# TensorE fed from the start, attention's two ends and the last row rearranged, in a hybrid decoder block

## The chip, the cores and the metric

The kernel runs on one core of one Trainium2 chip. The metric is the device time of one execution in microseconds; of several runs the median counts. The core has a matrix engine (TensorE, "PE" in the profile, with "PEld" for its loading of weights), three engines for element-wise work (VectorE "DVE", ScalarE "ACT", GpSimd "POOL") and a queue engine (SyncE "SP") that issues most of the transfers (DMA). Each engine works through its own list of instructions in order.

## The reference

One decoder block on x of 1024 positions by 1024 channels, all in float32. A conditioning vector c gives six modulation vectors (shift, scale and gate, twice). A normalised and modulated x is projected to an S5 input u, to q, k, v and to two gates; an S5 state-space branch and an attention branch run side by side, are merged by the gates, and a SwiGLU feed-forward part follows.

```
mod = silu(c) @ w_ada + b_ada                  -> sh1, sc1, g1, sh2, sc2, g2
h = rmsnorm(x, norm1_g) * (1 + sc1) + sh1
u, q, k, v, gate_a, gate_b = split(h @ w_in)
y_a = s5_branch(u) @ w_a                       # scan over 1024 steps, then a GLU
y_b = stick_breaking_attention(q, k, v) @ w_b
x = x + g1 * ((sigmoid(gate_a) * y_a + sigmoid(gate_b) * y_b) @ w_o)
h = rmsnorm(x, norm2_g) * (1 + sc2) + sh2
x = x + g2 * ((silu(h @ w_ffn_gate) * (h @ w_ffn_up)) @ w_ffn_down)
out = rmsnorm(x, norm_f_g)

# attention, 8 heads of 64; strictly causal
z = q @ k.T / 8 ;  mask = key < query
log_not = where(mask, log_sigmoid(-z), 0)
suffix  = sum of log_not over the later keys
weights = where(mask, exp(log_sigmoid(z) + suffix), 0)
out     = weights @ v
```

## The kernel before, in words

Most matrix products are done as three products of split operands: each float32 operand is cut into a high and a low part (the high part by a copy on ScalarE or GpSimd, the low part by a subtraction on VectorE or GpSimd), and TensorE adds high x high, high x low and low x high. Weights come in through `weight` (L442): a load, the two splits, and a ring of buffers (`wring`) whose next use has to wait for the products of the one before.

The work is written as a sequence of stages. A scheduler sets the order of the instructions on each engine by a simulated timeline; in the stage `start` the order is the written one, and in attention all matrix products are pinned to the written order (`pinned`, L832).

1. `start` (L563): SyncE loads x, the columns of w_in for u, and the first third of w_ada, in the order in which they are used. The row norms are worked out (`square`, `rstd`, `scale`); `turn` (L640) transposes x on TensorE against the identity; `small` transposes the small parameters; `ada_products` (L609) and `ada_sums` (L617) make the first modulation vectors, in four groups g of 256 columns: 32 products, a copy on ScalarE, and four products with one column. `modulate` turns the transposed x into h, and `product` forms u. The steps of the S5 parameters go on VectorE beside it.
2. The S5 branch, with the projection to v and gate_a on TensorE beside it, and the rest of w_ada multiplied by c on VectorE (`ada_rest`, L991), whose partial sums are stored to memory as `aD`.
3. The GLU of the S5 branch, the projections to q and k of the first pair of heads, and `branch_a` (L1070): product with w_a, times the sigmoid of gate_a (`gt`), result `na` stored as `nD`; the last of `ada_rest` runs beside it.
4. `attention` (L942). 40 units: four pairs of heads, two halves of the queries, and blocks of 128 keys from late to early. A unit has three steps: `scores` (L875: z = q k on TensorE, a mask addition on the diagonal ones on VectorE, a softplus on ScalarE and VectorE, split into `wh` and `wl`), `sums` (L906: suffix sums by products with a triangle and with ones, the running row kept in `row0` and `row1`; then an exponential), and `values` (L932). `scores` of a unit is written three units ahead (LOOK). Between the steps go single products of `fillers` (L836): the jobs in JOBS are the projections to q and k of the later pairs of heads and to gate_b, 48 products each, handed out 8 after the sums, 8 after the scores, and 12 after each of the first three scores (FILL). What is left over runs behind the last unit. A job's weights are loaded two jobs ahead (AHEAD). `triangles` (L818) builds the triangle and the mask on GpSimd just before attention.
5. `branch_b` (L1090): product with w_b, merge with gate_b and `nD`. Its accumulators go round eight PSUM banks (`banks`). `ada_row` spreads g1; `ada_cols` (L1022) makes the second shift and scale, 16 products with one column from `aD`.
6. `attend_out` (w_o, residual, second norm, transposes), and the feed-forward part `ffn` with `gate_up` and `down`, whose products are arranged as in Strassen's method.
7. The last rows (L1448 on): for each of eight blocks of 128 rows the last products, the residual, the sum of squares, and `close` (L1436), which takes the root (`rstd_p`, `rstd_s`) and scales the row. The last block is done in two halves: after the first half, two GpSimd steps (L1467) prepare the root and a third (L1468) multiplies the left half of the row by the norm's weights.

SBUF buffers come from pools that are laid out from the left and from the right. A new pool lies where closed ones lay, and its first writes wait for their last users. Before attention, the pools `tri` and `work` are opened after the stage `branch_a` has closed its pool `ar2`, which holds `gt`, `na` and the partial sums of `ada_rest`.

Of the kernel before, what the change touches and what calls it, by code (L numbers as in the profile page):

```python
# [365 lines left out]
KT = 8  # L366
# [12 lines left out]
FILL = (8, 8, 12)  # L379
JOBS = (("q", 1), ("k", 1), ("g", 0), ("g", 1), ("q", 2), ("k", 2), ("g", 2), ("q", 3), ("k", 3), ("g", 3), ("g", 4), ("g", 5), ("g", 6), ("g", 7))  # L380
# [49 lines left out]
class Block:  # L430
# [132 lines left out]
    def start(self, const, up, s5p):  # L563
# [8 lines left out]
        with self.pool("s0", 1, side="right") as sp, self.pool("s0a", 1, side="right") as ap, self.pool("s5t", 1, side="right") as st, \  # L572
# [66 lines left out]

            def turn(h, k):  # L640
                q = turned[h, k] = tp.tile([P, 512], F32, name="tp")
                for t in range(4):
                    nc.tensor.transpose(q[:, P * t:P * t + P], x[4 * h + t][:, P * k:P * k + P], self.ident)
# [192 lines left out]
    def fillers(self, qk, qp, kp, gp):  # L836

        nc = self.nc
# [4 lines left out]
        def load(j):  # L843
            n, i = jobs[j]
            c0 = {"q": 512, "k": 1024, "g": 3072}[n] + P * i
            loaded.append(self.w3(self.weight(self.in_cols(c0), lo_eng=nc.gpsimd, hi_eng=nc.gpsimd if n == "g" else None, ring=rings[j % 3])))
# [3 lines left out]
        for j, (n, i) in enumerate(jobs):  # L850
            if j + AHEAD < len(jobs):
                load(j + AHEAD)
            if n != "g":
                t = (qp if n == "q" else kp).tile([P, 1024], F32, name=n)
                qk[i][n == "k"] = t
# [19 lines left out]
    def scores(self, u, qk, work):  # L875
# [18 lines left out]
        if diag:  # L894
            m = P * (2 - len(u.kbs))
            nc.vector.tensor_tensor(a, z, self.mask[:, m:m + f].unsqueeze(1).broadcast_to([P, 2, f]), ALU.add)  # L896
        else:
            nc.scalar.copy(a, z)
# [43 lines left out]
    def attention(self, qk, qp, kp, vp, op, gp, work):  # L942
# [5 lines left out]
        for n in range(RWB):  # L948
            t = work.tile([P, 2, 512], F32R, name=f"row{n}")
            nc.vector.tensor_scalar(t.rearrange("p a (b c) -> p (a b) c", c=P), self.ident.unsqueeze(1).broadcast_to([P, 8, P]), 0.0, None, ALU.mult)  # L950
            carries.append(t)
# [6 lines left out]
        fill = self.fillers(qk, qp, kp, gp)  # L958
# [6 lines left out]
        for i in range(-LOOK, len(units) + 1):  # L965
# [56 lines left out]
    def ada_cols(self, const, tp, pp):  # L1022

        nc = self.nc
        ps = pp.tile([P, 512], F32, name="pa")
        for a in range(2):
            t = tp.tile([P, 1024], F32, name="ac")
            nc.sync.dma_start(out=t.rearrange("p (a b) -> p a b", a=2), in_=self.aD[:, 2 + 2 * a:4 + 2 * a])
            for k in range(KT):
                nc.tensor.matmul(ps[:, 8 * a + k:8 * a + k + 1], lhsT=t[:, P * k:P * k + P], rhs=self.ones[:, 0:1], start=True, stop=True)  # L1030
        self.mod2 = const.tile([P, 16], F32, name="mod2")
        self.G2 = const.tile([P, KT], F32, name="G2")
        nc.vector.tensor_tensor(self.mod2, ps[:, 0:16], self.cols[:, 88:104], ALU.add)
        nc.vector.scalar_tensor_tensor(self.G2, self.mod2[:, 8:16], 1.0, self.cols[:, 56:64], ALU.add, ALU.mult)


# [33 lines left out]
    def branch_a(self, y2p, tp, ap):  # L1070
# [3 lines left out]
        for c in range(4):  # L1074
# [3 lines left out]
            for m in (2 * c, 2 * c + 1):  # L1078
                for h in range(2):
                    s = slice(512 * h, 512 * h + 512)  # L1080
                    gt = ap.tile([P, 512], F32, name="gt", bufs=5)
# [4 lines left out]
                    o = ap.tile([P, 512], F32, name="na", bufs=5)  # L1086
# [3 lines left out]
    def branch_b(self, ops, const, tp, pa, spare, g1):  # L1090
# [4 lines left out]
        for c in range(4):  # L1095
            if c == 1:
                self.ada_row(g1, 0, tp, pa, ("ac", "pa"))
            if c == 2:
                self.ada_cols(const, tp, pa)
# [253 lines left out]
    def down(self, const, tp, g2):  # L1353
# [96 lines left out]
        for t in ROWS:  # L1450
# [3 lines left out]
            for c in range(2):  # L1454
# [8 lines left out]
                if t == ROWS[-1]:  # L1463
                    nc.scalar.activation(sq[:, cs], row[:, cs], AF.Square, accum_out=ss[:, c:c + 1])
                    if c == 0:
                        for n, f in ((4, 1.0), (5, -0.5)):
                            nc.gpsimd.tensor_scalar(small[:, t, n:n + 1], ss[:, 0:1], f / 1024.0, self.eps[:, n - 4:n - 3], ALU.mult, ALU.add)  # L1467
                        nc.gpsimd.tensor_tensor(row[:, cs], row[:, cs], gf[:, cs], ALU.mult)  # L1468
# [7 lines left out]
    def run(self):  # L1476
        tc, nc, i = self.tc, self.nc, self.i
        with ExitStack() as es:
# [20 lines left out]
            with ExitStack():  # L1499
# [21 lines left out]
                with ExitStack() as s3:  # L1521
                    with self.pool("ta", 2, side="right") as tp, \
# [15 lines left out]
                    with self.pool("tri", 1) as tri, self.pool("work", 1) as work, self.pool("zp", ZPB, PSUM) as self.zp, self.pool("acc", 1, PSUM) as self.accp, \  # L1538
                            self.pool("mx", MXB, PSUM) as mx:
                        self.avp = mg_  # L1540
                        self.triangles(tri)
                        self.mm = Turns((mm, "mm"), *[(mx, "mx")] * MXB)
                        qk = [list(qk[0])] + [[None, None] for _ in range(3)]
                        ops = self.attention(qk, qp, kp, vp, op, gp, work)
# [14 lines left out]
                    self.banks = Turns(*singles, *tpp.pools)  # L1559
                    mg = self.branch_b(ops, const, tp, self.banks, spare, g1)  # L1560
# [47 lines left out]
```

## Time and profile before

| | |
|---|---|
| timed runs | 1449.16, 1455.71, 1457.14 us; median 1455.71 |
| profiled execution | 1457.32 us |
| its span, first to last instruction | 1455.6 us |
| mean granted clock of TensorE | 0.986 |
| TensorE busy | 1408.4 us (97%) |
| VectorE busy | 1076.4 us (74%) |
| ScalarE busy | 640.4 us (44%) |
| GpSimd busy | 514.1 us (35%) |

The profile is one execution, and its times count from the first instruction. A line of the order of time gives the start, the busy time, the engine, the source line, the operation, output <- inputs, sizes and how many of them; in brackets how long the engine stood before it and for what. A line of the waits gives who waited for whom, the total in us, how often, and the longest. A line of a stretch gives the stretch, its length, the busy time of the engine or engines, the granted clock of TensorE as a share of full speed, the share of the DMA engines and GB/s. A DMA line gives its size and the median time from issue to landing. A float32 product that is not split appears as two records.

### The profile page before, as it was taken

To read this page: it belongs to the slowest core of one execution; us is meant where nothing else is said; L and a number is where in the kernel's file an instruction comes from. 1 tells how busy PE (TensorE), PEld (TensorE's weight loads), DVE (VectorE), ACT (ScalarE), POOL (GpSimd) and SP (SyncE) were. 2 spreads that over 40 slices of the span, in tenths; PEclk is the share of its full clock that TensorE was granted. 3 is DMA by queue.
4 is the path that set the end of the run, shared out by engine and by line. 5 is a ranking of instruction groups with operands and counts; after the bars stand their busy time and mean duration, and the time that the engine had idled before them with its cause. 6 is when DMAs were issued, how large, how long until landed. Compare 5 with 4: busy or idle time off the path is not lost. (4 is left out here: it accounts for less than half of the span.)

```text
span 1455.6 us, 18298 instructions
## 1 busy us (share of the span) xinstructions
PE 1408.4 (97%) x6730; PEld 1116.9 (77%) x6730; DVE 1076.4 (74%) x1395; ACT 640.4 (44%) x846; POOL 514.1 (35%) x291
## 2 busy tenths in 40 slices
PE   5999998999899999999999999999999999999997
PEld 3799887787666666658888888788888888788886
DVE  4779995456787889887723688777666667899896
ACT  3532112722586867674417543232323333433334
POOL 1010000102111022103400015876767566699394
PEclk9999999999999999999999999999999999999999
DMA  9665655489111112117452223644434369899722
GB/s 339 166 148 164 185 133 139 131 272 330 34 44 46 35 52 73 37 58 238 133 186 88 87 87 112 221 145 155 136 126 146 119 206 373 289 378 359 247 83 116
DMA packets 193561, 233.39 MB, mean 160 GB/s; under 512 B 29500, under 2 KB 128896, under 8 KB 193472
## 3 DMA queue, kind: packets, MB, share of 16 engines
q1 hardware_dynamic: 184336, 224.70, 47.1%
q10 hardware_dynamic: 8912, 7.48, 1.8%
q8 instruction: 53, 0.87, 0.2%
q14 instruction: 36, 0.29, 0.1%
q0 software_dynamic: 224, 0.05, 0.0%
HBM read 162.85 MB, written 68.16 MB: 159 GB/s over the span
## 5 line engine op out<-in xcount | busy, mean ns | idle before, releaser
L475 POOL TENSOR_TENSOR ws<-wb 128x1024 f32<-128x1024 f32 x24 | 60.7, 2527 | 175.8 <-DVE wl L478 148.1
L459 POOL TENSOR_TENSOR wl<-ws,wh 128x1024 fp32r<-128x1024 f32 x12 | 30.8, 2564 | 160.6 <-ACT wh L456 160.1
L927 DVE TENSOR_TENSOR wa<-wa,acc 128x512 f32<-128x512 f32 (+1 forms) x80 | 47.0, 628 | 32.9 <-ACT row L925 30.5
L1349 POOL TENSOR_TENSOR pa<-pa 128x512 f32<-128x512 f32 x30 | 63.4, 2143 | 0.3
L1293 POOL TENSOR_TENSOR f<-f,f 128x512 f32<-128x512 f32 x30 | 53.1, 1797 | 26.1 <-DVE f L1287 20.8
L899 ACT ACTIVATE ws<-wa 128x1024 f32<-128x1024 f32 (+1 forms) x40 | 39.1, 977 | 50.9 <-DVE wa L896 50.4
L904 DVE TENSOR_TENSOR wl<-ws,wh 128x1024 fp32r<-128x1024 f32 (+1 forms) x40 | 57.1, 1427 | 1.0
L478 DVE TENSOR_TENSOR wl<-ws,wh 128x1024 fp32r<-128x1024 f32 x23 | 41.4, 1798 | 20.2 <-ACT wh L477 20.1
L1004 DVE SCALAR_TENSOR_TENSOR acc<-aw,cond,acc 128x512 f32<-128x512 f32 x56 | 45.7, 816 | 10.2 <-DMA aw<-in_w_ada_dram 9.4
L456 ACT CAST wh<-ws 128x1024 fp32r<-128x1024 f32 x24 | 25.2, 1050 | 55.5 <-PE wo L1139 25.7
L902 DVE SCALAR_TENSOR_TENSOR ws<-wa,ws 128x1024 f32<-128x1024 f32 (+1 forms) x40 | 45.5, 1137 | 4.6 <-ACT ws L901 3.6
L834 PE MATMUL z<-q,k 64*128 64x512 f32 (+3 forms) x192 | 42.6, 534 | 6.1 <-DVE wa L896 4.9
L1378 POOL TENSOR_TENSOR pa<-pa,row 128x1024 f32<-128x1024 f32 x14 | 42.5, 3052 | 14.7 <-DMA pa<-in_w_ffn_down_dram 14.7
L1286 ACT ACTIVATE f<-f 128x1024 f32<-128x1024 f32 x20 | 21.2, 1061 | 59.5 <-DVE f L1324 30.8
L930 ACT ACTIVATE wa<-wa 128x1024 f32<-128x1024 f32 (+1 forms) x40 | 38.8, 971 | 19.3 <-DVE wa L927 18.3
L477 ACT CAST wh<-ws 128x1024 fp32r<-128x1024 f32 x23 | 24.1, 1054 | 50.9 <-PE wo L1302 15.6
L458 POOL TENSOR_SCALAR wh<-ws 128x1024 fp32r<-128x1024 f32 x6 | 7.5, 1245 | 105.0 <-issue 36.1
L477 ACT CAST wh<-wb 128x1024 fp32r<-128x1024 f32 x25 | 26.2, 1052 | 39.9 <-PE mm L1423 9.7
L475 POOL TENSOR_TENSOR wgs<-wb 128x1024 f32<-128x1024 f32 x12 | 28.9, 2405 | 40.8 <-DVE wl L478 19.9
L1423 PE MATMUL tq<-f,f 128*128 128x512 f32 x136 | 41.7, 389 | 0.0
L834 PE MATMUL mm<-wa,V 128*64 128x512 f32 (+3 forms) x192 | 39.8, 507 | 0.0
L478 DVE TENSOR_TENSOR wl<-wb,wh 128x1024 fp32r<-128x1024 f32 x25 | 38.1, 1528 | 1.9 <-ACT wh L477 1.9
(862 smaller groups left out, 4693.9 us busy)
## 6 DMA issues: line engine op xcount, KB each, us to landing
wb<-hD SPq DMA_DIRECT2D x40, 512.0 KB, 5.3
aw<-in_w_ada_dram SPq DMA_DIRECT2D x64, 256.0 KB, 4.3
hD<-f SPq DMA_DIRECT2D x30, 512.0 KB, 5.0
ws<-in_w_in_dram SPq DMA_DIRECT2D x23, 512.0 KB, 4.4
wb<-in_w_ffn_gate_dram SPq DMA_DIRECT2D x44, 256.0 KB, 4.2
wb<-in_w_ffn_up_dram SPq DMA_DIRECT2D x44, 256.0 KB, 4.6
ws<-hD SPq DMA_DIRECT2D x20, 512.0 KB, 4.8
x<-in_x_dram SPq DMA_DIRECT2D x16, 512.0 KB, 6.9
```

The costliest lines, as they stand in the source:

```text
L475: (add or nc.gpsimd).tensor_tensor(st, a, b, op)
L477: nc.scalar.copy(h, a)
L478: self.last_lo = (lo or nc.vector).tensor_tensor(l, a, h.bitcast(F32), ALU.subtract)
L834: return self.tc.keep_in_program_order(self.nc.tensor.matmul(*args, **kw))
L902: nc.vector.scalar_tensor_tensor(st, a, 0.0, st, ALU.max, ALU.add)
L904: nc.vector.tensor_tensor(lt, st, ht.bitcast(F32), ALU.subtract)
L927: nc.vector.tensor_tensor(a[:, x, 0:f], a[:, x, 0:f], r[:, x, 0:f], ALU.subtract)
L1004: nc.vector.scalar_tensor_tensor(acc, w[:, j], cj, acc, ALU.mult, ALU.add)
L1293: self.last_sum = nc.gpsimd.tensor_tensor(o, a, b, op)
L1349: self.after(nc.gpsimd.tensor_tensor(t[:, n], part(a), part(b), SIGN_B[i]), first)
L1378: self.after(nc.gpsimd.tensor_tensor(w, w, g2, ALU.mult), first)
L1423: nc.tensor.matmul(ps, lhsT=o[x][:, P * t:P * t + P], rhs=o[y][:, R], start=(j == 0), stop=(j == 3 * np_ - 1))
```

## The change

- `start`: a helper `idle(n)` issues n transposes of the identity into an accumulator that the first real product overwrites. 78 stand ahead of the first transposes of x, 4 ahead of the first modulation sums, 9 behind them.
- Attention's fillers: `ada_cols` goes. Its 16 one-column products become four jobs "a" of four steps, between the last gate jobs; each has its own 256 KB load into a pool of its own (`cp`), and VectorE adds the bias behind it. In the list of jobs they count for the loading ahead. A fourth number in FILL hands out six filler steps in each of the last three units, which have no scores any more.
- Attention's buffers: `triangles` is built before the projections to q and k; `gt` and `na` of `branch_a` get a pool `na`; attention has the pools `row`, `part` (`wh`, `wl`) and `work` (`wa`, `ws`) in this order. The two rows are zeroed behind the first mask addition instead of ahead of everything.
- The last row: the two small steps go from GpSimd to ScalarE, and the multiplication of the left half by the norm's weights goes from GpSimd to VectorE, at the head of `close`.
- `branch_b` begins its cycle of banks at the third.

```diff
-FILL = (8, 8, 12)
-JOBS = (..., ("g", 4), ("g", 5), ("g", 6), ("g", 7))
+FILL = (8, 8, 12, 6)
+JOBS = (..., ("g", 4), ("a", 0), ("g", 5), ("a", 1), ("g", 6), ("a", 2), ("g", 7), ("a", 3))
...
+            def idle(n):
+                for _ in range(n):
+                    nc.tensor.transpose(acc[3][:, 0:P], self.ident, self.ident)
...
             acc = [(self.mm, mp)[m // 2].tile([P, 512], F32, name="mm") for m in range(4)]
+            idle(78)
             for t in range(4):
                 square(t, t % 2 == 0)
...
+            idle(4)
             ada_sums(0)
+            idle(9)
             for g in range(4):
...
+            if n == "a":
+                t = cp.tile([P, 512], F32, name="ac", bufs=2)
+                nc.sync.dma_start(out=t, in_=self.aD[:, 2 + i])
+                loaded.append(t)
+                return
...
+            if n == "a":
+                ps = self.mm.tile([P, 512], F32, name="mm")
+                for k in range(4):
+                    self.pinned(ps[:, k:k + 1], lhsT=loaded[j][:, P * k:P * k + P], rhs=self.ones[:, 0:1], start=True, stop=True)
+                    if k == 3:
+                        s = slice(4 * i, 4 * i + 4)
+                        nc.vector.tensor_tensor(self.mod2[:, s], ps[:, 0:4], self.cols[:, 88 + 4 * i:92 + 4 * i], ALU.add)
+                        if i > 1:
+                            nc.vector.scalar_tensor_tensor(self.G2[:, 4 * i - 8:4 * i - 4], ...)
+                    yield
+                continue
...
+        u.parts = [part.tile([P, 2, 512], F32R, name=t) for t in ("wh", "wl")]
         u.a, s = (work.tile([P, 2, 512], F32, name=t, bufs=b) for t, b in (("wa", WAB2), ("ws", WSB)))
-        u.parts = [work.tile([P, 2, 512], F32R, name=t, bufs=WHB) for t in ("wh", "wl")]
...
-            t = work.tile([P, 2, 512], F32R, name=f"row{n}")
-            nc.vector.tensor_scalar(t..., self.ident..., 0.0, None, ALU.mult)
+            t = rowp.tile([P, 2, 512], F32R, name=f"row{n}")
...
             if i + LOOK < len(units):
-                self.scores(units[i + LOOK], qk, work)
+                self.scores(units[i + LOOK], qk, part, work)
+                if i == -LOOK:
+                    for t in carries:
+                        self.after(nc.vector.tensor_scalar(t..., self.ident..., 0.0, None, ALU.mult), self.masked)
                 some(FILL[1] if i >= 0 else FILL[2])
+            elif i < len(units):
+                some(FILL[3])
         some(10000)
...
             if t == ROWS[-1]:
+                nc.vector.tensor_tensor(row[:, L], row[:, L], gf[:, L], ALU.mult)
                 r = self.rstd_p(...)
...
                         for n, f in ((4, 1.0), (5, -0.5)):
-                            nc.gpsimd.tensor_scalar(small[:, t, n:n + 1], ss[:, 0:1], f / 1024.0, self.eps[:, n - 4:n - 3], ALU.mult, ALU.add)
-                        nc.gpsimd.tensor_tensor(row[:, cs], row[:, cs], gf[:, cs], ALU.mult)
+                            nc.scalar.activation(small[:, t, n:n + 1], ss[:, 0:1], AF.Identity, bias=self.eps[:, n - 4:n - 3], scale=f / 1024.0)
...
+                        self.triangles(s3.enter_context(self.pool("tri", 1)))
                         qk = [self.qk_proj(0, qp, kp, None)]
                         self.mm = Turns((ga, "ga"))
-                        with self.pool("ar2", 1, side="right") as ap:
-                            self.branch_a(y2p, tp, ap)
+                        with self.pool("na", 5, side="right") as np_, self.pool("ar2", 1, side="right") as ap:
+                            self.branch_a(y2p, tp, np_, ap)
...
-                    with self.pool("tri", 1) as tri, self.pool("work", 1) as work, ...
+                    with self.pool("row", 1) as rowp, self.pool("part", WHB) as part, self.pool("work", 1) as work, ...
...
                     self.banks = Turns(*singles, *tpp.pools)
+                    self.banks.n = 2
```

More of the change, by code (lines that the diff above doesn't have):

```diff
@@ L834, in pinned, with fillers @@
         return self.tc.keep_in_program_order(self.nc.tensor.matmul(*args, **kw))
-    def fillers(self, qk, qp, kp, gp):
-        nc = self.nc
+    def fillers(self, qk, qp, kp, gp, cp):
+        nc, turn = self.nc, 0
         rings = [self.wring[0], self.wring[0], self.wring[2]]
@@ L843, in load @@
         def load(j):
+            nonlocal turn
             n, i = jobs[j]
+            if n == "a":
[3 more added lines that the diff above has]
+                return
             c0 = {"q": 512, "k": 1024, "g": 3072}[n] + P * i
-            loaded.append(self.w3(self.weight(self.in_cols(c0), lo_eng=nc.gpsimd, hi_eng=nc.gpsimd if n == "g" else None, ring=rings[j % 3])))
+            loaded.append(self.w3(self.weight(self.in_cols(c0), lo_eng=nc.gpsimd, hi_eng=nc.gpsimd if n == "g" else None, ring=rings[turn % 3])))
+            turn += 1
         for j in range(AHEAD):
@@ L852, in fillers @@
                 load(j + AHEAD)
+            if n == "a":
[6 more added lines that the diff above has]
+                        if i > 1:
+                            nc.vector.scalar_tensor_tensor(self.G2[:, 4 * i - 8:4 * i - 4], self.mod2[:, s], 1.0, self.cols[:, 48 + 4 * i:52 + 4 * i], ALU.add, ALU.mult)
+                    yield
+                continue
             if n != "g":
@@ L873, in fillers, with scores @@
                         yield
-    def scores(self, u, qk, work):
+    def scores(self, u, qk, part, work):
         nc = self.nc
         q, k = qk[u.hp]
+        u.parts = [part.tile([P, 2, 512], F32R, name=t) for t in ("wh", "wl")]
         u.a, s = (work.tile([P, 2, 512], F32, name=t, bufs=b) for t, b in (("wa", WAB2), ("ws", WSB)))
-        u.parts = [work.tile([P, 2, 512], F32R, name=t, bufs=WHB) for t in ("wh", "wl")]
         z = self.zp.tile([P, 2, 512], F32, name="z")
@@ L895, in scores @@
             m = P * (2 - len(u.kbs))
-            nc.vector.tensor_tensor(a, z, self.mask[:, m:m + f].unsqueeze(1).broadcast_to([P, 2, f]), ALU.add)
+            self.masked = nc.vector.tensor_tensor(a, z, self.mask[:, m:m + f].unsqueeze(1).broadcast_to([P, 2, f]), ALU.add)
         else:
@@ L940, in values, with attention @@
             self.nc.scalar.copy(out[:, 512 * u.Q:512 * u.Q + 512], g.av)
-    def attention(self, qk, qp, kp, vp, op, gp, work):
+    def attention(self, qk, qp, kp, vp, op, gp, rowp, part, work, cp):
         nc = self.nc
@@ L957, in attention @@
                     units.append(Bag(hp=hp, Q=Q, kbs=kbs, group=g))
-        fill = self.fillers(qk, qp, kp, gp)
+        fill = self.fillers(qk, qp, kp, gp, cp)
         def some(n):
@@ L979, in attention @@
             if i + LOOK < len(units):
-                self.scores(units[i + LOOK], qk, work)
+                self.scores(units[i + LOOK], qk, part, work)
+                if i == -LOOK:
+                    for t in carries:
+                        self.after(nc.vector.tensor_scalar(t.rearrange("p a (b c) -> p (a b) c", c=P), self.ident.unsqueeze(1).broadcast_to([P, 8, P]), 0.0, None, ALU.mult), self.masked)
                 some(FILL[1] if i >= 0 else FILL[2])
+            elif i < len(units):
+                some(FILL[3])
         some(10000)
@@ L1020, in ada_row @@
             nc.vector.tensor_tensor(row[:, js], ps, row[:, js], ALU.add)
[L1022 to L1034, printed above, removed]
     def split(self, hi, lo, src, eng=None):
@@ L1068, in halves, with branch_a @@
         return [[t[:, :, k, 512 * h:512 * h + 512] for k in range(4)] for h in range(2)]
-    def branch_a(self, y2p, tp, ap):
+    def branch_a(self, y2p, tp, np_, ap):
         nc, i = self.nc, self.i
@@ L1097, in branch_b @@
                 self.ada_row(g1, 0, tp, pa, ("ac", "pa"))
-            if c == 2:
-                self.ada_cols(const, tp, pa)
             if c < 3:
@@ L1537, in run @@
                     op = s3.enter_context(self.pool("o", 4))
-                    with self.pool("tri", 1) as tri, self.pool("work", 1) as work, self.pool("zp", ZPB, PSUM) as self.zp, self.pool("acc", 1, PSUM) as self.accp, \
+                    with self.pool("row", 1) as rowp, self.pool("part", WHB) as part, self.pool("work", 1) as work, self.pool("zp", ZPB, PSUM) as self.zp, self.pool("acc", 1, PSUM) as self.accp, \
                             self.pool("mx", MXB, PSUM) as mx:
                         self.avp = mg_
-                        self.triangles(tri)
                         self.mm = Turns((mm, "mm"), *[(mx, "mx")] * MXB)
                         qk = [list(qk[0])] + [[None, None] for _ in range(3)]
-                        ops = self.attention(qk, qp, kp, vp, op, gp, work)
+                        with self.pool("cp", 1, side="right") as cp:
+                            ops = self.attention(qk, qp, kp, vp, op, gp, rowp, part, work, cp)
                         spare = []
```

9 lines of the change are left out of this document (5 added, 4 removed).

## The prediction

> **What bounds the kernel now.** I read the page first, for each engine's share of the span, then TensorE's list of waits, then the busy time by stretches with the granted clock, and last the order of time at the places those two named.
>
> ```profile
> span 1455.6 us, 18298 instructions
> PE 1408.4 (97%) x6730; PEld 1116.9 (77%) x6730; DVE 1076.4 (74%) x1395; ACT 640.4 (44%) x846; POOL 514.1 (35%) x291
> PE s5a L354 <- DMA gD<-gst: 4.9, 1, 4.9
> 367.50:370.00 2.50, 1.21 (x4) 0.54 0.00 0
> 370.00:372.50 2.50, 2.50 (x7) 0.50 0.01 3
> 372.50:375.00 2.50, 2.50 (x8) 0.59 0.00 0
> ```
>
> TensorE is busy for 97% of the span, so there are only two things to win: the 47 us in which it does nothing, and the stretches in which it is busy at half speed. The stretch rows (the stretch, its length, TensorE's busy time, matmuls, granted clock) show the second kind: after the idle time before 368.8 the clock stands near 0.5, and 2.5 us hold 7 or 8 matmuls. Added up, (1 - 0.54)/0.5 x 2.5 + 2.5 + (1 - 0.59)/0.5 x 2.5 gives 6.9 us of half speed, 3.4 us lost, beside the idle time itself. Four of the five groups of edits sit at such a place, the fifth is the tail. What lies between them goes on at TensorE's pace and shifts as a whole, so a microsecond won there should arrive at the end. The 4.9 us before L354 is not touched: VectorE's chain of the S5 part sets it, and that chain starts behind the first stage, so it shifts too.
>
> The profiled execution took 1457.3 us, 1.7 more than its span. The three timed runs have their median at 1455.7, 1.6 lower, and spread over 8 us.
>
> **The start.** 78 transposes of the identity are put ahead of the first real ones, 4 and 9 more into the two gaps around the first modulation sums.
>
> ```profile
> 2.25 0.31 POOL masks.py:199 TENSOR_SCALAR_AFFINE_SELECT ident<-ident 128x128 f32<-128x128 f32 x1
> 13.69 2.17 PE L643 MATMUL tp<-ident,x 128*128 128x128 f32 x8 [13.69 <-ACT x L636]
> 15.66 0.21 DVE L557 COPY rows<-ld 16x128 f32<-16x128 f32 x1
> 16.78 3.27 PE L989 MATMUL mm<-pb,cond 128*32 128x256 f32 x32 [0.38 <-DVE cols L561]
> 20.77 1.05 PE L621 MATMUL adap<-ones,acc 128*128 128x1 f32 x8 [0.71 <-ACT acc L615]
> 23.08 0.80 PE L660 MATMUL mm<-pa,wh 128*128 128x512 f32 x1 [1.26 <-ACT pa L649]
> 24.65 1.22 PE L660 MATMUL mm<-pa,wh 128*128 128x512 f32 x2 [0.35 <-DVE pa L654]
> 26.65 3.46 PE L989 MATMUL mm<-pb,cond 128*32 128x256 f32 x32
> 46.72 1.93 PE L989 MATMUL mm<-pb,cond 128*32 128x256 f32 x32
> 83.90 1.04 PE L217 MATMUL tp<-ident,cl 128*128 128x128 f32 x8
> 84.73 0.39 PE L781 MATMUL mm<-wh,pa 128*128 128x256 f32 x1
> L606 SPq DMA_DIRECT2D pb<-in_w_ada_dram x16: 368/926/4552, 3.7 to 34.8; - x16
> pb<-in_w_ada_dram SPq DMA_DIRECT2D x1, 512.0 KB, 9.1
> ```
>
> The same 32 products take 3.27 and 3.46 us in the first two groups and 1.93 in the last: until 30 us TensorE runs at half speed. A transposition at full speed is (84.73 - 83.90)/8 = 0.104 us, at half 0.208. The identity is there at 2.56. If the clock rises once, after the 6.9 us that half speed lasted at 368, 33 fillers are slow and 45 fast: 6.9 + 4.7, so they end at 14.2. The real transposes cannot start before 13.69, and then need 0.8 us instead of 2.17, done by 15.1; what comes next on TensorE waits for VectorE's copy that ends at 15.87. So the 78 cost nothing. At full speed the stage then wins 1.34 (3.27 - 1.93), 1.53 (3.46 - 1.93), 0.1 in the sums, 0.2 in the transposition ahead of the first group, and in the six products from 23.08 to 26.65 the part behind VectorE's low half: 3.57 becomes 1.57 + 4 x 0.227 = 2.5, 1.1 won. Together 4.3. The stage's loads do not undo that: the last quarter of the weights is issued at 34.8 and lands 9.1 later, at 43.9; products of 46.72 moved up by 4.3 reach their last quarter at 43.9. Behind it the products follow without a gap. I take 3.5, because TensorE is nearly empty from 14 to 16.6 and the clock may fall once more; the bounds are 2 (one such fall) and 4.3. The 13 small fillers go into gaps of 0.71 and 1.26: 4 x 0.104 and 9 x 0.104 fit.
>
> **Attention's start.** The triangles and the mask are now built before the first q and k; the buffers lie in pools of their own, so that the scratch tiles no longer wait for the last store of the stage before; the zeroing of the two carry rows moves behind the first mask addition.
>
> ```profile
> 359.87 2.80 DVE L1004 SCALAR_TENSOR_TENSOR acc<-aw,cond,acc 128x512 f32<-128x512 f32 x1
> 360.01 0.93 PE L834 MATMUL z<-q,k 64*128 64x128 f32 x8 [1.18 <-DVE na L1087]
> 365.34 2.01 DVE L950 TENSOR_SCALAR row<-ident 128x1024 fp32r<-128x1024 f32 x2 [2.67 <-DMA aD<-acc]
> 367.78 0.96 DVE L896 TENSOR_TENSOR wa<-z,mask 128x768 f32<-128x768 f32 x1 [0.20 <-POOL mask L830]
> 368.79 1.65 PE L834 MATMUL z<-q,k 64*128 64x384 f32 x4 [4.91 <-DVE wa L896]
> 373.03 0.96 DVE L904 TENSOR_TENSOR wl<-ws,wh 128x768 fp32r<-128x768 f32 x1
> 379.15 0.33 PE L834 MATMUL acc<-wh,upto 128*128 128x384 f32 x1
> 1276.51 7.25 PE tq L1423 x32
> ```
>
> The scores are ready at 361, but the mask addition stands until 367.78 behind GpSimd's mask, and VectorE, whose zeroing comes first, stood itself until a store of the stage before had landed at 365.3. Without it VectorE is free at 362.67, when its last modulation step ends: 5.1 us sooner. TensorE then has twelve filler products until 363.9, the addition is done at 363.6, and nothing stands. From 360.01 to the first sums at 379.15 TensorE has three score groups (0.9 each) and 36 fillers at 7.25/32 = 0.227: 10.9 us of work in 19.1, so up to 8.2 to win, the half speed included. VectorE's side: from the end of the first addition (368.74) to that of L904 (373.99) are 5.25 us; with the zeroing (2.0) and the second addition (0.96) laid between, it is done by some 371, where TensorE wants it at 370.9. The zeroing may stand for the last store of the stage before, and the second mask addition is queued behind it on VectorE, which the third score group waits for: up to 1 us. I take 7.2, between 5.1 (only the first addition's gain stays, the rest goes at VectorE's pace) and 8.2. The wait of 1.18 stays.
>
> **Attention's end and the modulation sums.** The 16 sums with one column, so far a block in the next stage, become four jobs of four among the fillers, and the last three units get six fillers each.
>
> ```profile
> 643.58 0.50 PE L834 MATMUL acc<-wh,upto 128*128 128x512 f32 x1 [1.34 <-DVE row L929]
> 649.26 0.50 PE L834 MATMUL acc<-wh,upto 128*128 128x512 f32 x1 [1.19 <-DVE row L929]
> 682.29 4.21 PE L1030 MATMUL wo<-ones,ac 128*128 128x1 f32 x32
> 686.36 1.20 PE L1118 MATMUL wo<-V,wh 128*128 128x512 f32 x2
> 691.62 0.79 PE L1118 MATMUL tq<-V,wh 128*128 128x512 f32 x2
> ```
>
> The block costs more than its own 4.1 us. The twelve products from 686.36 to 691.62 take 5.26 us where 12 x 0.227 is 2.7: 2.6 lost to half speed, with TensorE never idle. A quarter of the block is 1 us, like the group of eight records at 20.77, of which there is one behind each group of 32 products; the last 32 take the full-clock 1.93 all the same. So I take the 2.6 as won, with nothing as the lower bound. The 4.1 itself only moves. The six fillers are 1.36 us each time against gaps of 1.34 and 1.19: 2.2 won, between 0.5 and 2.5. Eighteen filler steps are left behind the last unit where there were twenty, enough for the last head's split; the shifted bank order I cost at nothing, since the products from 686.36 on stand back to back, with 0.5 as its bound either way.
>
> **The last row.**
>
> ```profile
> 1447.36 1.58 POOL L1467 TENSOR_SCALAR ss<-ss,eps 128x1 f32<-128x1 f32 x2
> 1448.74 0.29 ACT L510 ACTIVATE ss<-ss 128x1 f32<-128x1 f32 x1 [0.86 <-POOL ss L1467]
> 1448.91 1.25 POOL L1468 TENSOR_TENSOR pa<-pa,gf 128x512 f32<-128x512 f32 x1
> 1450.15 0.26 POOL L512 TENSOR_SCALAR ss<-ss 128x1 f32<-128x1 f32 x1
> 1451.26 0.72 ACT L1439 ACTIVATE pa<-pa,ss 128x512 f32<-128x512 f32 x1 [1.98 <-POOL ss L514]
> ```
>
> GpSimd's 1.58 and 1.25 are on the path: ScalarE stands 0.86 for the first, and the root's GpSimd steps begin at 1450.15, behind the second. Now ScalarE, free at 1448.74 - 0.86 = 1447.88, does two small steps of its own (0.29, as L510) and the root's first, until 1448.75; from there the rest goes as today, 1451.26 - 1450.15 = 1.1, and ends at 1449.86. The multiplication goes to VectorE, 2/3 of L896's 0.96 or 0.64; I take it as hidden behind the root, and uncovered it costs that. I take 1.4, between 0.7 and 1.6.
>
> Sum: 3.5 + 7.2 + 2.6 + 2.2 + 1.4 = 16.9, so 1440.4 by the profiled execution, and 1440 as the median.
>
> **The rivals.** *The fillers do not raise the clock* (0.20). No row shows a long run of transposes on a slow TensorE, and what the array counts as work is not plain: in the block at 682 it was busy all the time and the clock fell. Then 78 x 0.208 = 16.2 us end at 18.8, the eight real ones at 20.5 where the next step now starts at 15.9: 4.6 lost, 0.6 more as nine slow fillers (1.9) overfill 1.26. The start is 5.2 worse instead of 3.5 better: 1449. [...]
>
> *VectorE sets attention's pace* (0.13).
>
> ```profile
> 380.00:400.00 20.00, 20.00 (x102) 14.28 (x101) 18.41 (x22) 11.48 (x15) 4.01 (x2) 1.00 0.09 27
> ```
>
> Here, where TensorE, its loads, VectorE, ScalarE and GpSimd stand in this order, VectorE is busy for 18.4 of 20 us. Then the start of attention keeps only 5.1 and the end gives nothing: 1457.3 - 3.5 - 5.1 - 2.6 - 1.4 = 1445. Against it: TensorE is busy for all 20 of them.
>
> *Gate weights come too late* (0.05), the slower side. The four sum jobs stand in the same list as the weight loads, two ahead; at its end the weights for three gate jobs are now asked for one product job ahead, not two. (The sums' own loads come from what was stored before attention, and nothing hurries them.)
>
> ```profile
> 363.12 25.49 SPq L449 DMA_DIRECT2D ws<-in_w_in_dram  x2
> ws<-in_w_in_dram SPq DMA_DIRECT2D x23, 512.0 KB, 4.4
> ```
>
> A gate job is 48 products, 16 to a unit; a unit takes (649.26 - 379.15)/39 = 6.9, a job 20.8 us. Were each load held in SyncE's queue for 25.5 us as here, it would land 25.5 + 4.4 - 20.8 = 9.1 late; TensorE's order is fixed, and sums and scores stand behind the filler: 27 us for three, 1468. It turns slower than before once a load is held over 22 us (5.6 late, three times). Against it: this long hold is that of the refill behind attention's start, where nothing was urgent.
>
> **How the numbers follow.** Forecast 0.62, the rivals 0.20, 0.13, 0.05. The range goes from 1435 (all upper bounds: 4.3 + 8.2 + 2.6 + 2.5 + 1.6 off 1457.3 give 1438, and the runs' median lies 1.6 below the profile and may fall a little further) to 1450, which takes in the first two rivals and leaves out some 0.15. About 0.5%, 7.3 us, is what a measurement of this kernel can tell from no change: the line lies at 1448.4. The forecast, the second rival and half of the first lie below it: 0.85 faster; half of the first 0.10 the same; 0.05 slower.
>
> **What would show it.** Right: in the first 30 us the second group of 32 products near 2 us; the list of TensorE's waits without the 4.9 at L834; first sums some 15 us after the first scores; no clock near 0.5 after the modulation sums; the last row's scaling on ScalarE beginning 1.4 sooner behind the last product. Wrong: the first real transposes at 18 us or later; new waits of TensorE for weights in attention.

## The result, and the profile after

The median of eight runs is 1443.2 us (1440.9 to 1445.9); the kernel before, in eight runs beside them, has 1453.2 (1448.0 to 1457.1). The ratio is 0.9934, with a 95% interval of 0.9914 to 0.9954: some 10 us won, and 1440 was forecast. Between the two profiled executions it is 1457.3 against 1440.9, 16.4, which is almost the sum of 16.9 that the prediction made. This agreement is in part an accident, as the landmarks show (us from the span's start; the third and fourth kernel come with the experiments):

| landmark | before | changed | changed, again | lead_kept |
|---|---|---|---|---|
| first product on the second half's columns (`mm<-pb`) | 62.26 | 63.37 | 61.96 | 59.09 |
| first product of the gelu stage (`ga<-yp`) | 264.88 | 265.50 | 264.61 | 261.13 |
| first scores (`z<-q,k`) | 360.01 | 356.64 | 359.15 | 351.23 |
| first sums (`acc<-wh,upto`) | 379.15 | 368.73 | 371.19 | 363.27 |
| first product of the output projection (`tq<-wh,pa`) | 710.88 | 695.47 | 698.05 | 690.03 |
| end of the last product | 1446.06 | 1430.37 | 1434.28 | 1425.27 |
| span | 1455.6 | 1439.2 | 1443.1 | 1434.1 |

From row to row, the changed kernel won -1.1 (the start), 0.5, 4.0 (the gelu stage, which the change does not touch), 7.1 (attention's start), 5.0 (attention's end and the sums), 0.3 and 0.7 (the last row): 16.4. The start, forecast at 3.5, lost; the gelu stage, forecast at nothing, made up for it.

First the page of the changed kernel.

```profile
span 1439.2 us, 18486 instructions
PE 1409.5 (98%) x6821; PEld 1122.9 (78%) x6821; DVE 1079.8 (75%) x1400; ACT 640.7 (45%) x848; POOL 515.6 (36%) x288
```

TensorE is busy as long as before (1408.4 there), though some 13 us of fillers (the transpositions of the identity: 11.0 for the 78, 0.7 and 1.2 for the two small groups) are now among it: all else it does takes some 12 us less, being at half speed in fewer places (mean granted clock 0.995, 0.986 before). Its idle time went from 47 us to 30, mostly by those fillers. Then two of the first rows of TensorE's list of waits (us in total, times, longest).

```profile
PE s5a L354 <- DMA gD<-gst: 4.7, 1, 4.7
...
PE mm L664 <- ACT pa L653: 2.4, 2, 2.2
```

The 4.9 at attention's start and the 3.7 at its end are gone from the top; what is new is a wait of 2.2 in the first stage. The order of time of the engines there, as the changed kernel has it:

```profile
2.61 11.01 PE L642 MATMUL mm<-ident 128*128 128x128 f32 x78 [2.61 <-POOL ident masks.py:199]
16.44 1.93 PE L1018 MATMUL mm<-pb,cond 128*32 128x256 f32 x32 [0.38 <-DVE cols L561]
24.10 1.98 PE L1018 MATMUL mm<-pb,cond 128*32 128x256 f32 x32
36.00 2.05 SPq L591 DMA_DIRECT2D ws<-in_w_in_dram  x1
42.99 1.93 PE L1018 MATMUL mm<-pb,cond 128*32 128x256 f32 x32
45.30 1.05 ACT L596 CAST u3h<-ws 128x1024 fp32r<-128x1024 f32 x1 [3.75 <-DMA ws<-in_w_in_dram]
47.31 0.56 ACT L615 COPY acc<-mm 128x512 f32<-128x512 f32 x1
52.74 0.16 DVE L624 TENSOR_TENSOR mod<-adap,cols 128x4 f32<-128x4 f32 x1
54.02 0.50 PE L664 MATMUL mm<-pa,u3h 128*128 128x512 f32 x1 [2.19 <-ACT pa L653]
63.37 0.48 PE L664 MATMUL mm<-pb,wh 128*128 128x512 f32 x1
```

The fillers take 11.0 us, the groups of 32 products 1.93 and 1.98 where they took 3.27 and 3.46, and the fourth group begins at 42.99 instead of 46.72. There the lead ends. ScalarE's next step in its order is the cast of u3, the last quarter of this stage's own weights, and it stands 3.75 for the load. That load was issued at 36.00. In the kernel before both came at the same times:

```profile
36.05 2.06 SPq L591 DMA_DIRECT2D ws<-in_w_in_dram  x1
45.41 1.05 ACT L596 CAST u3h<-ws 128x1024 fp32r<-128x1024 f32 x1 [0.23 <-DMA ws<-in_w_in_dram]
48.73 0.59 ACT L615 COPY acc<-mm 128x512 f32<-128x512 f32 x1 [1.22 <-PE mm L989]
62.26 0.48 PE L660 MATMUL mm<-pb,wh 128*128 128x512 f32 x1
```

Behind the cast and a sum of squares the copy of the fourth group comes at 47.31, 1.4 sooner than before; behind VectorE's sums of squares and angles the modulation comes at 52.74, 0.2 sooner. TensorE, now early, has nothing to do meanwhile, and the clock falls (the stretch, its length, TensorE's busy time, matmuls, granted clock, DMA share, GB/s):

```profile
51.69:55.10 3.41, 0.88 (x3) 1.00 0.95 312
55.10:58.51 3.41, 2.92 (x7) 0.50 0.02 8
```

At attention's start, its end and the last row the changed kernel did what was forecast:

```profile
356.64 0.93 PE L841 MATMUL z<-q,k 64*128 64x128 f32 x8 [0.95 <-DVE na L1101]
360.97 0.92 PE L841 MATMUL z<-q,k 64*128 64x384 f32 x4 [0.44 <-DVE wa L921]
368.73 0.33 PE L841 MATMUL acc<-wh,upto 128*128 128x384 f32 x1
629.70 0.95 PE L841 MATMUL mx<-ones,ac 128*128 128x1 f32 x8
639.92 0.49 PE L841 MATMUL acc<-wl,upto 128*128 128x512 f32 x1 [0.50 <-DVE wl L929]
1429.98 0.39 PE L1473 MATMUL mm<-wh,wl 128*128 128x512 f32 x1
1432.65 0.97 POOL L512 TENSOR_SCALAR ss<-ss 128x1 f32<-128x1 f32 x1 [1.00 <-ACT ss L1480]
1434.46 0.72 ACT L1452 ACTIVATE pa<-pa,ss 128x512 f32<-128x512 f32 x1 [1.49 <-POOL ss L514]
```

The first sums stand 12.1 behind the first scores (19.1 before), the second score group waits 0.44, a quarter of the sums is 0.95 long, a wait of 0.50 is left at attention's end, and the last scaling begins 4.1 behind the last product's end (5.2 before). In the kernel before, the clock was near 0.5 from 685 to 692, behind the block of sums. In the changed kernel no stretch from 660 to 700 is below 1.00; one of them, with the busy times of TensorE, its loads, VectorE, ScalarE and GpSimd ahead of the clock:

```profile
685.00:687.50 2.50, 2.50 (x12) 2.07 (x12) 2.50 (x4) 1.16 (x2) 1.27 (x2) 1.00 0.59 217
```

### The profile page after: what moved, and what is told of

Same layout as the page of the kernel before. It is cut to its first block, busy times and chain, and to the rows that moved or that the text cites. A ratio compares the mean times of both kernels' runs of the same rounds, so it can differ in the third digit from the quotient of the medians.

```text
span 1439.2 us, 18486 instructions
## 1 busy us (share of the span) xinstructions
PE 1409.5 (98%) x6821; PEld 1122.9 (78%) x6821; DVE 1079.8 (75%) x1400; ACT 640.7 (45%) x848; POOL 515.6 (36%) x288
## 4 chain that ended last, share of the span: by engine, by line
PE 71%; DVE 10%; DMA 8%; issue 4%; ACT 3%; POOL 3%; SPq 1%; POOLq 0%; DVEq 0%; ACTq 0%
PE tq L1314 9%; PE tq L1435 6%; PE wo L1314 5%; PE mm L1314 5%; PE mx L841 5%; PE mm L841 5%; PE mm L767 3%; PE mm L1435 3%; PE wo L1435 3%; PE ga L767 3%; PE acc L841 2%; PE wo L1151 2%; PE mm L1151 2%; PE mm L664 2%; PE z L841 2%
## 5 line engine op out<-in xcount | busy, mean ns | idle before, releaser
L478 DVE TENSOR_TENSOR wl<-ws,wh 128x1024 fp32r<-128x1024 f32 x23 | 40.8, 1772 | 19.1 <-ACT wh L477 19.1
```

The source lines that it names most:

```text
L478: self.last_lo = (lo or nc.vector).tensor_tensor(l, a, h.bitcast(F32), ALU.subtract)
```

## The experiments

Theory 1: the start's lead is lost at u3 and in ScalarE's and VectorE's order behind it; the gain is that of attention's start, its end, the sums and the last row. Theory 2: the start brings its 3.5, and the others less than their profile shows. All times below stand beside runs of the kernel before on the same chip.

**start_only**: the kernel before with `idle(78)`, `idle(4)`, `idle(9)` alone.

> The kernel before with the 78, 4 and 9 transpositions of the identity alone. Theory 1 (the start's lead is lost at the last part of the stage's weights, u3, whose load lands at 45.3 whatever TensorE does, and in ScalarE's and VectorE's order behind it): the second group of 32 products takes 2.0 us and stands 2.5 us earlier, yet the first product on the second half's modulated columns (pb) begins at 62 to 63.5, as in the kernel before (62.3), and the time is that of the kernel before, 1453, or up to 2 more. Theory 2 (the 3.5 us of my sum arrive, and the profile after only fell into a low clock at 55 by chance): pb begins at 59, and the time is 1449.7.

Median 1450.6, ratio 0.9972 (0.9955 to 0.9989). Its first product on pb comes later still, behind a gap of 2.16 and a low clock from 55 to 62:

```profile
65.13 0.47 PE L664 MATMUL mm<-pb,wh 128*128 128x512 f32 x1
366.43 0.92 PE L841 MATMUL z<-q,k 64*128 64x384 f32 x4 [2.45 <-DVE wa L903]
```

So the start lost 2.9 in this profile. What it won came elsewhere: the unchanged code at attention's start had a wait of 2.45 instead of 4.91 and kept its clock (1.00 in every row of 2.5 us from 360 to 390), 14.1 from the first scores to the first sums instead of 19.1. VectorE's last modulation step took 0.74 there, 2.80 in the profile before. The time alone would speak for theory 2: the kernel before has a median of 1455.7 on this chip, 5.1 more. The landmarks put the gain elsewhere, so the mechanism of theory 1 holds; its time was 3 too high.

**rest_only**: the changed kernel without the three `idle` calls.

> The changed kernel without the 78, 4 and 9 transpositions of the identity. Theory 1 (the start brings nothing, all of the gain comes from attention's start, its end and the last row): 1442 to 1443.5, as the changed kernel; the groups of 32 products take 3.3 to 3.5 us again, and the first product on pb begins near 62.3. Theory 2 (the start brings 3.5): 1446.7.

Median 1445.1, ratio 0.9934 (0.9914 to 0.9953), the changed kernel's own ratio; pb begins at 62.29, between the 61.96 and 63.37 of the changed kernel's two profiles. The time alone, 1.5 to 1.9 over the changed kernel's medians on other chips, lies between the theories; the landmark decides for the first.

**lead_kept**: the same work of the first stage in another order, in short form:

```
+ if g == 2: square(4..7)            # ahead of the split of u3
  product, ada_products(3), turns
+ ada_sums(3); u_split(3); rstd      # was: u_split(3), squares, S5 step, rstd, ada_sums(3)
+ next(steps)                        # behind the scaling of rows 4 to 7
```

> The changed kernel with the same work of the first stage in another order: the sums of squares of rows 4 to 7 go ahead of the split of u3, the split, the root of those sums and the S5 step behind the last modulation sums. Theory 1 (ScalarE's and VectorE's order behind u3's load holds the stage's end): the copy of the last group's products no longer stands for u3, the first product on u3 begins near 49.5 instead of 54.0, TensorE's gap ahead of it and the low clock at 55 are gone, pb begins at 58 to 59, the wait ahead of L354 stays near 4.7, and the time is 1438, 5 less than the changed kernel. Rival (the loads themselves, or the S5 chain behind, set the end): u3's products still begin at 53 or later, or the wait ahead of L354 grows by what was won, and the time stays 1443.

```profile
45.10 0.59 ACT L615 COPY acc<-mm 128x512 f32<-128x512 f32 x1 [1.20 <-PE mm L1017]
45.59 1.05 ACT L596 CAST u3h<-ws 128x1024 fp32r<-128x1024 f32 x1
48.27 0.17 DVE L624 TENSOR_TENSOR mod<-adap,cols 128x4 f32<-128x4 f32 x1 [3.35 <-PE adap L621]
51.06 0.51 PE L664 MATMUL mm<-pa,u3h 128*128 128x512 f32 x1
```

The cast still begins at 45.6, but the modulation comes at 48.27, 4.5 sooner, and TensorE goes on to u3 without a gap. pb begins at 59.09 and the end moves with it: median 1437.0, ratio 0.9879 (0.9854 to 0.9903). The first product on u3 came at 51.1, 1.6 later than I expected. This version beats both kernels, the changed one by comparison with runs on other chips (1443.2 and 1443.5).

**order_only**: lead_kept without the transpositions.

> The reordered kernel (lead_kept) without the 78, 4 and 9 transpositions. Theory 1 (the transpositions' 3 to 4 us arrive only where the order behind u3's load lets them, and the order alone has little to win, as the last group of 32 products ends at 48.6, behind u3): the first product on u3 at 54, pb near 62, as in rest_only; 1444 to 1445, some 7 more than lead_kept. Rival (the order alone carries what lead_kept won): pb near 59 to 60, 1438 to 1440.

Median 1447.1, ratio 0.9947 (0.9931 to 0.9963); pb at 62.67. The order alone wins nothing, the transpositions alone next to nothing, both together 8 against rest_only, which ran on lead_kept's chip: 3.2 of them at pb, the others where lead_kept had a shorter low clock ahead of the gelu stage (3.4 us, 6.8 in rest_only) and none in it (6.8 in rest_only). Only the 3.2 can be put down to the first stage; the others are where the clock happened to stay up (warm and lead_glu, below, begin as early and do not have them).

**sums_block**: the sixteen sums as one block again, no "a" jobs, banks as before.

> The changed kernel with the sixteen modulation sums as one block in the next stage again, the order of banks there as before. Theory 1 (a block of 32 records with one column lets the clock fall, quarters of it do not): the block takes 4.1 us, some 6.8 us at a clock near 0.5 follow it, and with 3.4 us of quarters gone from attention the time is 3.3 more than the changed kernel's, 1446.5. Rival (the low clock behind the block was chance): no low clock behind it, and the time is 1444.

```profile
669.50 3.63 PE L1092 MATMUL wo<-ones,ac 128*128 128x1 f32 x32
675.38 0.63 PE L1147 MATMUL wo<-oh,wl 128*128 128x512 f32 x1
```

Median 1444.7, ratio 0.9928 (0.9905 to 0.9952). Behind the block one product takes 0.63 again where 0.39 is usual: the low clock came back, though for 3.4 us, not 6.8; from the first sums to the output projection's landmark it took 328.3 against 326.7 in the changed kernel. Theory 1's mechanism holds, with half its price in this execution; the median is nearer to the rival's 1444 than to 1446.5.

**no_fill**: `FILL = (8, 8, 12, 0)`.

> The changed kernel with no fillers at the last three units of attention; the 18 products left over run behind the last unit. Theory 1 (the six fillers stand in gaps of 1.2 to 1.3 us): waits of TensorE for VectorE's row of 1.2 to 1.4 at the last two units come back, some 2.0 more from the last scores to the first products of the output projection, 1445.5. Rival (the fillers delay what they fill): no more than 0.5.

```profile
635.12 0.50 PE L841 MATMUL acc<-wh,upto 128*128 128x512 f32 x1 [1.43 <-DVE row L954]
640.70 0.50 PE L841 MATMUL acc<-wh,upto 128*128 128x512 f32 x1 [1.07 <-DVE row L954]
```

Median 1446.5, ratio 0.9941 (0.9924 to 0.9957). Both waits are back; from the last scores to the landmark of the output projection it takes 73.8 instead of 71.1. TensorE's waits in between add up to 3.5 instead of 0.5: besides these two there are 0.75 for `wl`, the low half from VectorE (0.50 in the changed kernel), and 0.24 for ScalarE's `wa`.

**changed_again**: no edit.

> The changed kernel unchanged, on the chip of the kernels beside it. Theory 1 (the granted clock changes only on a free-running grid of some 3.4 us, so equal gaps of TensorE lose the clock in one execution and keep it in another): time 1443; between the first scores and the first sums 12.1 again; the cast of u3 begins at 45.3 again and a gap of 2.2 stands ahead of its first product; but the low clocks at 55 and at 236 may be missing or longer, and one may come at the start of the gelu stage (269), which is worth up to 4 each. Rival (each low clock belongs to its gap): the low clocks of the first profile, at the same places with the same lengths.

Median 1443.5, ratio 0.9921 (0.9898 to 0.9944). Its profile has the low clock in the gelu stage that the first profile had not: from that stage's first product to the first scores 94.5, as in the kernel before (95.1), not 91.1. The low clock at 55 is missing in turn, though the gap there is 1.88, nearly as long: low clocks come and go between executions, as theory 1 said. The start is level there (61.96), and 7.1 and 4.9 are won at attention's two ends: 12.5 between the spans, where the medians of this chip, 1455.7 and 1443.5, give 12.2.

**pools_back**: the tiles `gt`, `na`, `row`, `wh`, `wl` in the pools that they had; triangles early, zeroing late.

> The changed kernel with the gate and product tiles of the stage before, the carry rows and the split halves in the pools that they had; the early triangles and the late zeroing stay. Theory 1 (order alone: mask early, zeroing late): 12 to 12.5 from the first scores to the first sums, time as the changed kernel. Rival (the pools: a scratch tile of attention lies where a tile of the stage before is still being stored): VectorE's first mask addition or the zeroing stands for that store, a wait of 2 to 5 of TensorE at the second or third score group, 3 to 7 more.

```profile
365.88 0.96 DVE L921 TENSOR_TENSOR wa<-z,mask 128x768 f32<-128x768 f32 x1 [5.31 <-DMA aD<-acc]
366.90 1.65 PE L841 MATMUL z<-q,k 64*128 64x384 f32 x4 [5.81 <-DVE wa L921]
```

Median 1451.6, ratio 0.9973 (0.9958 to 0.9988): 8.0 over changed_again on the same chip. The mask is ready, the zeroing is behind, and still VectorE stands 5.31 for the store of `acc`, since its target lies where `acc` lay. From the first scores to the first sums it takes 19.4. The rival holds, 1.0 beyond its 3 to 7: the pools carry the gain.

**zero_first**: the zeroing written ahead of the first unit.

> The changed kernel with the zeroing of the two carry rows ahead of the first mask addition again; triangles, mask and pools stay as changed. Theory 1 (with pools of their own the rows wait for no store, and the mask is ready long before): the zeroing's 1.3 to 2.0 us on VectorE come ahead of the first mask addition, from the first scores to the first sums 13.5 to 14 instead of 12.1, time 1.5 more than the changed kernel. Rival (it is the order that won it, the zeroing still stands for the last store): a wait of 2 to 5 of TensorE ahead of the second score group, 15 to 19 from the first scores to the first sums, 3 to 7 more.

Median 1443.1, ratio 0.9916 (0.9892 to 0.9940), 12.3 from scores to sums. VectorE still ran the mask addition first (362.89) and the zeroing second (363.76): the edit did not reach the engine's order, so the order's worth is not tested.

**warm**: lead_kept with 40 transpositions ahead of L354.

> The reordered kernel (lead_kept) with 40 transpositions of the identity more, 4.2 us at full clock, in TensorE's gap of 4.8 ahead of L354. Theory 1 (transpositions keep the clock as they raise it): no low clock at 232 to 245 any more, where the profiles so far had 3.4 to 6.8 us of it; the product steps behind it take half the time; TensorE's wait there is 0.6; 1.7 to 3.4 off, 1434 to 1435. Rival (they only fill: the clock falls as before, or they delay the S5 products by their own time at half speed): 1437 or up to 4 more.

```profile
229.73 4.53 PE L352 MATMUL s5a<-ident 128*128 128x128 f32 x40
234.68 0.46 PE L356 MATMUL s5a<-u,tz 128*128 128x128 f32 x2 [0.41 <-DMA gD<-gst]
240.11 0.72 PE L768 MATMUL mm<-pa,wgh 128*128 128x512 f32 x2 [1.62 <-ACT wgh L458]
```

The clock stays up (1.00 in the rows from 230.0 to 237.5, products of 0.39 behind) and the wait is filled, as theory 1 said, yet the median is 1441.6, ratio 0.9906 (0.9883 to 0.9928), 4.6 over lead_kept (on another chip, whose median for the kernel before is the same 1455.7). The next products now wait 1.62 for their weights; the gelu stage begins 202.3 behind pb's first product, where lead_kept took 202.0. Then that stage, with 3.9 us of waits and a low clock (products of 0.63 instead of 0.39), took 94.2 to the first scores against lead_kept's 90.1. So the filled wait was paid for elsewhere, for the most part in a stage that the edit does not touch.

**glu_warm** and **lead_glu**: 14 transpositions in the first product group of the gelu stage, in the changed kernel and in lead_kept.

> The changed kernel with 14 transpositions of the identity in the first product group of the gelu stage, where TensorE stands 2.0 to 2.6 in all for ScalarE's split and its clock fell in five of the eight profiles of kernels with the old order of the first stage. Theory 1 (the gap costs by the clock that it loses, not by itself): no low clock at 270 to 280, from the stage's first product to the first scores 91 to 92 instead of 94.5, the median 1 to 3 less than the changed kernel's 1443.5 and its runs closer together. Rival (the transpositions stand in the way of products that are ready): 94 or more, 1443.5 to 1445.

> The reordered kernel (lead_kept) with the same 14 transpositions in the gelu stage. Theory 1: where lead_kept keeps its clock there already, nothing is left to win but its slower executions: 1436 to 1437. Rival (they stand in the way): 1437 to 1439.

```profile
268.76 0.38 PE L767 MATMUL ga<-ident 128*128 128x128 f32 x2
270.81 0.80 PE L769 MATMUL ga<-yp,wh 128*128 128x512 f32 x1 [1.67 <-ACT yp L1054]
271.40 1.27 PE L767 MATMUL ga<-ident 128*128 128x128 f32 x5
```

Medians 1446.1 (0.9940, 0.9922 to 0.9957) and 1442.0 (0.9911, 0.9893 to 0.9930): both lie above even the rivals' ranges (to 1445 and to 1439), so theory 1 fails in both. From the stage's first product to the first scores they took 96.5 and 94.3, with a low clock there (products of 0.63 instead of 0.39 in both). These rows of glu_warm show why: only two of the fourteen stood in TensorE's order ahead of the gap of 1.67, the others behind it, ahead of products that were ready. Whether well-placed ones would pay is open.

## Why the prediction was right, and where it was wrong

**The start** (forecast 3.5, measured -1.1, and 0.3 in the second profile). Its first half held: the fillers raised the clock. The rows of 2.5 us hold 11 and 15 of them from 2.5 to 7.5, and 26 behind that. (The clock's column reads 1.00 from the start, also where a transposition takes twice as long; here the counts tell the speed.)

```profile
2.50:5.00 2.50, 2.39 (x11) 1.00 0.87 285
5.00:7.50 2.50, 2.50 (x15) 1.00 1.02 406
7.50:10.00 2.50, 2.50 (x26) 1.00 1.03 377
```

The 78 end at 13.6, where 14.2 was forecast, and the fourth group of 32 products begins 3.7 sooner: up to there the sum is right. The lower bound had its reason too: in sums_block's profile, with the same fillers, the clock fell once more behind them; TensorE was busy for 1.11 of the 2.5 us from 12.5, and the clock reads 0.62 from 15.0 to 17.5 and 0.50 from 17.5 to 25.0. In the changed kernel's first profile it reads 1.00 there, behind 2.17 of 2.5. The first rival falls. The step that failed is "The stage's loads do not undo that … Behind it the products follow without a gap". I checked the `pb` loads alone. The load of u3 stands behind them in SyncE's queue, is issued at 36.0 in both kernels and lands at 45.3. A TensorE that is 3.7 us early meets an in-order ScalarE that stands for that load, with the copy TensorE needs queued behind. lead_kept shows that the order was the fault: the load is issued at the same time (36.06), its cast begins at 45.59, and the lead arrives. The other profiles agree. pb begins at 62.3 without fillers, at 62.7 with the new order alone, at 61.9 to 65.1 in the eight profiles with the fillers in the old order, and at 58.8 to 60.1 in the three with both.

**Attention's start** (7.2, measured 7.1 in both profiles, 8.0 by the medians with and without the pools). Sum and bounds were right. Of its causes the prediction named pools, early mask and late zeroing together; the pools carry the gain, the early mask without them nothing. With them it may count, for in the kernel before GpSimd's first step on the triangle stood for the same store:

```profile
365.35 0.20 POOL L822 MEMSET tri<- 128x128 f32 x1 [3.22 <-DMA aD<-acc]
```

Without that wait the mask, 2.4 of work, would have been ready at 364.5, still 1.9 behind VectorE's 362.67. This is an estimate; no run had the pools without the early mask. The up to 1 us for the zeroing did not come. The last paragraph's "some 15 us" from scores to sums was a slip against its own sum (19.1 - 7.2 = 11.9); 12.1 came. The 4.9 that was removed is not constant either: start_only's profile had 2.45.

**The sums** (2.6) **and attention's end** (2.2): 5.0 together in the profile, for the two and the quarters' smaller time. Apart, sums_block gives 1.6 with one low stretch of 3.4 (by estimate 1.7 more had it been 6.8, as before), no_fill 2.8.

**The last row** (1.4): the scaling begins 1.1 sooner, and 0.7 of it reaches the span's end, as the stores behind took 4.0 instead of 3.6. The mis-sized term is the root's first GpSimd step: 0.26 in the profile before, 0.97 in the one after, so that from it to the scaling it takes 1.8 instead of 1.1.

```profile
1430.30 0.27 POOL L512 TENSOR_SCALAR ss<-ss,eps 128x1 f32<-128x1 f32 x1 [1.52 <-ACT ft L1484]
1432.89 0.68 DVE L1450 TENSOR_TENSOR pa<-pa,gf 128x512 f32<-128x512 f32 x1
```

GpSimd's wait of 1.00 ahead of it is not the reason: one block of rows earlier the same line took 0.27 behind a wait of 1.52. The slow step ends at 1433.62, 0.05 behind the end of the multiplication that the change moved to VectorE; in the kernel before VectorE had no work at that time. So the multiplication was probably not hidden behind the root, and costs 0.7, about the 0.64 that the prediction put on it "uncovered". No run took it away, so this is not shown.

**The bank order** (0) was not tried alone. The one new wait near it, 0.83 at 707.57, is for VectorE's half of a weight and not for a bank, and rest_only, with the same bank order, has none there.

**The rivals.** VectorE did not set attention's pace: the 7.1 and the end's gain both came. No wait for gate weights appears.

**The total.** The 16.9 met the 16.4 of the profiles because the missing 4.6 of the start were made up by 4.0 in the gelu stage. Its low clock, 6.8 us in the profile before, is in seven of the twelve profiles with that stage untouched (products of 0.63 instead of 0.39; in pools_back and warm 3.4 us of it), and not in the other five. By the medians the gain is 10 and 12, so the sum was 5 to 7 too large. The forecast of 1440 came out only 3 low, about the size of the term that failed, because the kernel before has 1453.2 in eight runs and not the 1455.7 of the first three: that part is luck.

## What to carry to other kernels

Before an engine's lead is counted, follow every load of the stage to its landing and list, on each in-order engine, what stands behind the step that waits for it: a lead is lost at the first such step, unless an order that puts the ready work first goes with it. Here neither won anything alone, and together they won some 3 us. Where the first tile of a stage waits for a store of the stage before, give the tiles addresses of their own; here reordering what uses them, without that, won nothing. A gap that costs the clock in one profile may not in the next (ahead of u3's first product 2.19 us did, 1.88 in the second profile of the same kernel did not), so a gain at such a place wants several executions, and landmarks rather than the total.

## What the runs showed of the hardware

In the profiles of the kernel before and of the changed kernel the granted clock changes on a grid of 3.41 us. Up to the last product it falls to 0.50 at 22.97, 234.60, 268.73, 367.71 and 685.15 in the one, for 6.83 us each time, and at 55.10 (for 3.41) and 236.00 (for 6.83) in the other. From 234.60 the next three lie 34.13, 133.11 and 450.55 away, 10, 39 and 132 times 3.413, and 236.00 lies 180.90, 53 times, behind 55.10. From the span's start 234.60 is 68.73 such steps and 55.10 is 16.14, so the grid is not tied to it. Cut on the grid, the rows of the kernel before are purely 1.00 or 0.50 (stretch, its length, TensorE's busy time, clock):

```profile
231.19:234.60 3.41, 1.16 (x6) 1.00 0.53 65
234.60:238.01 3.41, 0.75 (x3) 0.50 0.71 185
238.01:241.43 3.42, 3.42 (x18) 0.50 1.08 306
265.31:268.73 3.42, 0.91 (x3) 1.00 0.56 192
268.73:272.14 3.41, 2.84 (x6) 0.50 0.66 191
```

The clock fell behind stretches in which TensorE was busy for 1.16, 0.91 and (changed kernel, at 51.69) 0.88 of 3.41. In the changed kernel's gelu stage the gaps fell otherwise across the grid, and the emptiest stretch had 1.92:

```profile
266.72:270.14 3.42, 1.92 (x8) 1.00 0.61 211
```

There the clock stayed. Cut in this way from 19.55 us to the last product, these two profiles have six falls behind stretches at 1.00 in which TensorE was busy for 0.00 to 1.55 of 3.41, and one behind a stretch full of one-column sums, busy for all 3.41 (at 681.74, before); behind every other stretch at 1.00, the emptiest the one with 1.92, the clock stayed. Behind the blocks of sums in start_only and sums_block it fell too, to 0.50 from 680.0 to 685.0 and from 675.0 to 677.5. That a gap of some 2 us costs the clock or not by where it lies on the grid is the author's estimate from these rows; no run moved a gap alone. Why the gelu stage's waits differ by 2 us between executions of almost the same code was not settled.
